# A two-layer trunk on one core: other order of small steps in attention, other queues at the start, other parts at the end

## The chip, the cores and the metric

The program runs on one core of a Trainium2 chip. The metric is device time in microseconds (us), from the first to the last instruction with what lies around them, as the median of several runs. TensorE multiplies matrices into PSUM, VectorE and ScalarE compute elementwise, GpSimd does small jobs and issues some transfers, and SyncE (SP) issues most transfers.

## The reference

Two layers over x of 256 tokens and 2048 features, all float32:

```python
for i in range(2):
    h = rms_norm(x, norm_gains[i])
    y = hgrn2_mixer(...) if i == 0 else nsa_mixer(...)
    x = x + y
return rms_norm(x, final_gain)
```

The first mixer is a gated linear recurrence with 16 heads of 128. The second is an attention with 16 heads in 4 groups and three branches (compressed, selected and window keys) whose outputs are weighted by learned gates and multiplied by silu(z). With 256 tokens there are four blocks to select from and all are taken. Each mixer has one wide input projection (2048 to 8192, and to 7216) and an output projection of 2048 x 2048. The lower bound of the first mixer's forget gate is a softmax over three rows of `hgrn_lb`.

## The kernel before, in words

**Weights.** All projections go through one loop, `flush`, over a list of pieces. A piece is a weight block of up to 128 x 1024 numbers that SP loads (`emit_load`), ScalarE casts to a rounded part hi (line 138) and VectorE subtracts to a part lo (line 148). TensorE multiplies with three products instead of one, hi times hi, hi times lo and lo times hi (lines 156, 179 and 181), so that the sum is close to float32. hi runs up to four pieces ahead of the products (`SPLIT_AHEAD`), lo three; there are four buffers of each and six of raw weights.

**Small steps.** Everything else is written as Python generators. `run` appends one to the list `steps`; `advance` gives each in the list's order one turn, up to its next `yield`. `flush` calls `advance` twice a piece, before and after its products. So a `yield` is a half step, and the order of a half step's instructions on an engine is the order of the list. Engines run their instructions in the order in which they are written; a wait holds up all that is behind it.

**Attention.** `attend(g)` handles the four heads of a group; four of them are appended to the list when the last query chunk of group 0 is done, each with a later start. A head takes four pieces: `logits` after the products of the first (three PSUM banks), `biased` and `exps` in the second, `weigh` in the third, `transposes` and `evacuate` after the products of the fourth. `transposes` fills two banks: t1 with four 128 x 128 blocks, t2 with two and the compressed branch's 47 rows. `evacuate` (lines 997 to 1012) casts the blocks to ph on ScalarE (line 1004), copies the compressed rows to pc (line 1006), and on VectorE forms the second parts pl (line 1008) and the rest of pc (lines 1009 and 1011). After two heads `values` multiplies: in one piece with the blocks of t1 and, in its last product (line 1029), with pc; in the next piece with the other blocks. The four auxiliary banks go round: for the first pair of heads of a group the next head's logits are written before the value products and both take banks that t1 and t2 held; for the second pair the value products come first.

Beside it the projections go on. A chunk of queries (`q_split`: qh on ScalarE, line 854, then ql on VectorE) or of gates (`gated`: Silu on ScalarE, line 1073, then an Exp of one column at line 1076, so that Exp's table is loaded again) ends at about the half step before an odd head's transposes.

**Start.** `load_x` loads x in eight blocks of 256 columns. The blocks and the first six weight pieces are issued by SP in turns; the two layers' gains gn by ScalarE ahead of all. TensorE runs idle products (`keep_busy`) on a tile of zeros, transposes the gains (line 1196), and x's blocks one by one (line 339); ScalarE and VectorE split x into two parts (lines 342 and 345), scaled by the gains. In the first pieces the transposes of a later x block stand between the products of an earlier piece. `setup` builds masks, the bias rows and, in its last part, the lower bounds: VectorE's lbe, an Exp on ScalarE (line 429) and five small VectorE operations.

**End.** The last 256 columns are kept back so that the first 128 tokens are finished (`finish`, lines 1156 to 1169) while TensorE still works on the other 128. `finish` adds the residual, sums squares, takes the root on GpSimd, scales x2 by it in parts, and stores three parts: 512 columns from ScalarE's queue, 512 and 1024 from SP's.

Of the kernel before, what the change touches and what calls it, by code (L numbers as in the profile page):

```python
# [8 lines left out]
F32 = mybir.dt.float32  # L9
# [3 lines left out]
AF = mybir.ActivationFunctionType  # L13
ALU = mybir.AluOpType
AX = mybir.AxisListType

P = 128
D = 2048
# [27 lines left out]
def kernel(ctx: ExitStack, tc: tile.TileContext, x, norm_gains, final_gain, rel_bias,  # L46
# [20 lines left out]
        return psa.tile([P, 512], F32, tag="aux", name="auxps")  # L67

    gn = const.tile([32, P], F32, name="gn")
    nc.scalar.dma_start(gn, norm_gains.rearrange("a (h d) -> (a h) d", d=P))  # L70
    ident = const.tile([P, P], F32, name="ident")
    make_identity(nc, ident)
    nc.scalar.activation(ident[:, 0:1], ident[:, 0:1], AF.Identity)
    mhalf = const.tile([P, 8], F32, name="mhalf")
    nc.gpsimd.memset(mhalf, -0.5)

# [248 lines left out]

    def load_x(c):
        cs = slice(c * 256, (c + 1) * 256)
        nc.sync.dma_start(xt[:, :, cs], x_rows[:, cs].rearrange("(t p) c -> p t c", p=P))

    def split_x(kts):  # L330
        if kts[0] % 2:
# [41 lines left out]
    def setup():  # L373
# [51 lines left out]
        nc.vector.tensor_max(lbm, lb3[:, 0], lb3[:, 1])  # L425
        nc.vector.tensor_max(lbm, lbm, lb3[:, 2])
        nc.vector.tensor_sub(lbe, lb3, lbm[:, None, :].to_broadcast([P, 3, NH]))
        yield
        nc.scalar.activation(lbe, lbe, AF.Exp)
        lbs = sp.tile([P, NH], F32, name="lbs")  # L430
# [487 lines left out]
        return done  # L918

    def q_split(g, a, q):  # L920
        NS["q", g, a] = [NS["p2"].tile([P, 2, S], F32R, tag="q" + part, name="q" + part, bufs=3) for part in "hl"]
        yield from split_of([q], *([t] for t in NS["q", g, a]))

# [7 lines left out]
    def attend(g):  # L931
# [64 lines left out]
        def evacuate(h):  # L996
            t1, t2 = L.pop(("t", h))
            a, hh = h // 2, h % 2
            ph, pl = pT[a]
            srcs = ((t1.rearrange("p (a t) -> p a t", a=4), slice(0, 4)),  # L1000
                    (t2[:, 0:256].rearrange("p (a t) -> p a t", a=2), slice(4, 6)))
            pc = NS["pc"][:, hh]
            for t, ks in srcs:
                nc.scalar.copy(ph[:, ks, hh, :], t)  # L1004
            for tt in range(2):
                nc.scalar.copy(pc[64:64 + NCMP, tt], t2[32 * tt:32 * tt + NCMP, 256:384])  # L1006
            for t, ks in srcs:
                nc.vector.tensor_sub(pl[:, ks, hh, :], t, ph[:, ks, hh, :].bitcast(F32))  # L1008
            nc.vector.tensor_copy(pc[0:NCMP], pc[64:64 + NCMP].bitcast(F32))
            for tt in range(2):  # L1010
                nc.vector.tensor_sub(pc[32:32 + NCMP, tt], t2[32 * tt:32 * tt + NCMP, 256:384],  # L1011
                                     pc[64:64 + NCMP, tt].bitcast(F32))

        def values(a, half):
            if half == 0:
# [53 lines left out]

    def gated(g, zs):  # L1070
        ks = [slice(4 * g + 2 * a, 4 * g + 2 * a + 2) for a in range(2)]
        for a in range(2):
            nc.scalar.activation(zs[a], zs[a], AF.Silu)  # L1073
        if g + 1 < G:

            nc.scalar.activation(NS["one"], NS["one"], AF.Exp, scale=0.0)
        yield
        yield
        for a in range(2):
            while ("out", g, a) not in NS:  # L1080
                yield
            nc.vector.tensor_mul(zs[a], zs[a], NS["o", g][:, a])
            yield
            yield
            nc.scalar.copy(yh[:, ks[a]], zs[a])
            yield
            nc.vector.tensor_sub(yl[:, ks[a]], zs[a], yh[:, ks[a]].bitcast(F32))
# [68 lines left out]
    def finish(tt, ps):  # L1156
        ms, x2, fg = FN["ms"][:, tt], FN["x2"][:, tt], FN["fg"]
        nc.vector.tensor_add(x2[:, 1792:], ps, res["x1", 4][:, tt])
        nc.vector.tensor_tensor_reduce(out=FN["sq"][:, :256], in0=x2[:, 1792:], in1=x2[:, 1792:], op0=ALU.mult,
                                       op1=ALU.add, scale=1.0 / D, scalar=ms[:, 0:1], accum_out=ms[:, 1:2])  # L1160
        nc.gpsimd.tensor_tensor(ms[:, 2:3], ms[:, 1:2], mhalf[:, :1], op=ALU.pow)
        rows, rs = out_rows[tt * P:(tt + 1) * P], ms[:, 2:3]
        nc.scalar.activation(x2[:, 0:512], x2[:, 0:512], AF.Copy, scale=rs)
        nc.vector.tensor_scalar(x2[:, 512:1024], x2[:, 512:1024], rs, None, op0=ALU.mult)
        nc.scalar.dma_start(rows[:, 0:512], x2[:, 0:512])
        nc.sync.dma_start(rows[:, 512:1024], x2[:, 512:1024])
        nc.vector.tensor_scalar(x2[:, 1024:1792], x2[:, 1024:1792], rs, None, op0=ALU.mult)
        nc.vector.scalar_tensor_tensor(x2[:, 1792:], x2[:, 1792:], rs, fg[:, 1792:], op0=ALU.mult, op1=ALU.mult)
        nc.sync.dma_start(rows[:, 1024:], x2[:, 1024:])

    def mean_so_far():
        for tt in range(2):
# [10 lines left out]
    nc.gpsimd.memset(prow, 0.0)  # L1183
    for c in range(8):
        load_x(c)
        for i in ((0, 1) if c == 0 else (c + 1,)):
            if i < RAW_BUFS:
                loaded[i] = emit_load(i)
    state["load"] = RAW_BUFS
    gp = aux_bank()  # L1190
    def keep_busy(n, m):
        for _ in range(n):
            nc.tensor.matmul(gp[:, 256:256 + P], m, m, start=True, stop=True)
# [2 lines left out]
    nc.tensor.transpose(gp[:, :32], gn, ident[:32, :32])  # L1196
    nc.vector.tensor_copy(gcol, gp[:, :32])
    start_piece(0)
    keep_busy(6, ident)
    run(setup())  # L1200
    run(norm_x())
    flush()
# [32 lines left out]
```

## Time and profile before

| | us |
|---|---|
| median of 3 runs (lowest to highest) | 986.13 (985.73 to 987.29) |
| the profiled execution | 986.4 |
| its span, first to last instruction | 984.6 |
| TensorE matmuls busy | 968.7 |
| TensorE weight loads busy | 838.5 |
| VectorE busy | 658.3 |
| ScalarE busy | 569.5 |
| GpSimd busy | 59.9 |

The profile is of one execution. A busy time is the union of an engine's instructions. Matmuls are pipelined and shown longer than the distance at which they start, so a TensorE that is shown as busy can still lose some time. In a row of the timeline the number in brackets is the time for which the engine stood idle before the instruction, with what ended it. The granted clock of TensorE is 0.998 of full speed over the span. Transfers move 178.98 MB, 182 GB/s on average.

### The profile page before, as it was taken

What the parts mean: (1) busy time and instruction counts of PE and PEld (TensorE: products, weight loads), DVE (VectorE), ACT (ScalarE), POOL (GpSimd) and SP (SyncE); (2) the same over time, 40 slices, a digit from 0 to 9 for tenths busy, and PEclk for the clock granted to TensorE, in tenths of its full rate; (3) what the DMA queues carried; (4) which work ended last, traced back from release to release, by engine and by line L of the source; (5) the groups of instructions that cost most, each with busy time, mean ns of one, the idle gap of its engine ahead of it and who ended that gap; (6) DMA issues with size and microseconds to landing.
All of it is one profiled execution on the core that took longest, in us unless ns stands there. A gap on an engine that the chain in (4) does not pass through costs nothing.

```text
span 984.6 us, 17622 instructions
## 1 busy us (share of the span) xinstructions
PE 968.7 (98%) x6735; PEld 838.5 (85%) x6735; DVE 658.3 (67%) x1275; ACT 569.5 (58%) x1056; POOL 59.9 (6%) x154
## 2 busy tenths in 40 slices
PE   9999999999999999999999999999999999999996
PEld 8888888888888888888888888998888888888886
DVE  6796478646864786465566666567777778686654
ACT  6754565456545654554455555467677776875542
POOL 3101000100010001000020000000000000000000
PEclk9999999999999999999999999999999999999999
DMA  9655565556555655566777776565555545546662
GB/s 317 201 172 151 172 192 165 157 171 193 156 166 172 186 158 163 176 222 231 234 218 207 223 229 184 157 198 170 150 152 141 158 130 160 160 130 232 204 215 96
DMA packets 141524, 178.98 MB, mean 182 GB/s; under 512 B 6016, under 2 KB 102880, under 8 KB 141312
## 3 DMA queue, kind: packets, MB, share of 16 engines
q1 hardware_dynamic: 139424, 171.86, 56.8%
q0 software_dynamic: 1680, 5.46, 2.0%
q8 instruction: 53, 0.87, 0.4%
q10 hardware_dynamic: 336, 0.54, 0.1%
q14 instruction: 31, 0.25, 0.1%
HBM read 173.62 MB, written 4.22 MB: 181 GB/s over the span
## 4 chain that ended last, share of the span: by engine, by line
PE 80%; ACT 10%; DVE 6%; issue 2%; DMA 1%; SPq 0%; POOLq 0%; ACTq 0%; POOL 0%; DVEq 0%
PE mainps L156 40%; PE mainps L179 21%; PE mainps L181 11%; PE auxps L156 3%; ACT L L970 2%; ACT hi L138 2%; PE auxps L516 2%; DVE lo L148 1%; DVE L L963 1%; ACT ph L1004 1%; ACT L L979 1%; ACT pc L1006 1%; DMA xt<-in_x_dram 1%; DVE pc L1011 1%; ACT L1073 1%
## 5 line engine op out<-in xcount | busy, mean ns | idle before, releaser
L179 PE MATMUL mainps<-xx,hi 128*128 128x512 f32 x1280 | 454.9, 398 | 0.2 <-DVE Kg L313 0.2
L138 ACT CAST hi<-raw 128x1024 fp32r<-128x1024 f32 (+3 forms) x317 | 328.0, 1039 | 206.6 <-PE mainps L156 142.8
L148 DVE TENSOR_TENSOR lo<-raw,hi 128x1024 fp32r<-128x1024 f32 (+3 forms) x317 | 379.2, 1206 | 92.1 <-ACT hi L138 91.3
L181 PE MATMUL mainps<-xx,lo 128*128 128x256 f32 x1280 | 357.6, 279 | 0.1
L179 PEld LDWEIGHTS mainps<-xx,hi 128*128 128x128 f32 x1280 | 240.2, 188 | 54.6 <-DVE Kg L313 0.6
L181 PEld LDWEIGHTS mainps<-xx,lo 128*128 128x128 f32 x1280 | 241.4, 189 | 0.6 <-DVE lo L148 0.4
L156 PE MATMUL mainps<-hi,xx 128*128 128x512 f32 (+1 forms) x704 | 209.4, 375 | 0.0
L156 PEld LDWEIGHTS mainps<-hi,xx 128*128 128x128 f32 x704 | 128.4, 188 | 23.2
L156 PE MATMUL mainps<-lo,xx 128*128 128x512 f32 (+1 forms) x352 | 131.0, 372 | 0.0
L156 PE MATMUL mainps<-hi,yh 128*128 128x512 f32 (+1 forms) x288 | 106.0, 368 | 0.0
L156 PE MATMUL mainps<-hi,yl 128*128 128x512 f32 (+1 forms) x288 | 105.4, 366 | 0.0
L156 PE MATMUL mainps<-lo,yh 128*128 128x512 f32 (+1 forms) x288 | 105.3, 366 | 0.0
L156 PEld LDWEIGHTS mainps<-lo,xx 128*128 128x128 f32 x352 | 66.1, 188 | 10.4
L156 PEld LDWEIGHTS mainps<-hi,yl 128*128 128x128 f32 x288 | 54.3, 189 | 8.8
L156 PEld LDWEIGHTS mainps<-lo,yh 128*128 128x128 f32 x288 | 54.4, 189 | 8.5
L156 PEld LDWEIGHTS mainps<-hi,yh 128*128 128x128 f32 x288 | 54.4, 189 | 8.4
L970 ACT ACTIVATE L<-L,mx 128x128 f32<-128x128 f32 (+1 forms) x96 | 37.6, 393 | 31.0 <-DVE mx L965 31.0
L313 DVE TENSOR_TENSOR zs<-mainps,zs 128x256 f32<-128x256 f32 x48 | 19.0, 421 | 33.7 <-ACT zs L311 33.7
L567 POOL COPY ST<-S 32x128 f32<-32x128 f32 x32 | 21.6, 675 | 229.8 <-DVE S L524 228.8
L524 DVE COPY_PREDICATED S<-masks,auxps 128x128 f32<-128x128 uint32 x48 | 14.6, 303 | 28.8 <-PE auxps L557 15.9
L1008 DVE TENSOR_TENSOR pl<-auxps,ph 128x512 fp32r<-128x512 f32 (+1 forms) x32 | 17.7, 557 | 22.0 <-ACT ph L1004 20.4
L311 ACT COPY zs<-mainps 128x256 f32<-128x256 f32 x48 | 16.5, 373 | 13.5 <-PE mainps L181 13.2
(257 smaller groups left out, 905.2 us busy)
## 6 DMA issues: line engine op xcount, KB each, us to landing
raw<-in_hgrn_w_in_dram SPq DMA_DIRECT2D x127, 512.0 KB, 4.0
raw<-in_nsa_w_in_dram SPq DMA_DIRECT2D x104, 512.0 KB, 3.8
raw<-in_hgrn_w_out_dram SPq DMA_DIRECT2D x32, 512.0 KB, 4.7
raw<-in_nsa_w_out_dram SPq DMA_DIRECT2D x32, 512.0 KB, 4.0
raw<-in_nsa_w_in_dram SPq DMA_DIRECT2D x10, 420.0 KB, 3.9
xt<-in_x_dram SPq DMA_DIRECT2D x8, 256.0 KB, 7.9
raw<-in_x_dram SPq DMA_DIRECT2D x4, 512.0 KB, 4.2
x_dram<-x POOLq DMA_DIRECT2D x4, 512.0 KB, 6.0
```

The source lines that it names most:

```text
L138: nc.scalar.copy(hi[:, :m], raw[:, :m])
L148: nc.vector.tensor_sub(lo[:, :m], raw[:, :m], hi[:, :m].bitcast(F32))
L156: nc.tensor.matmul(dst, a, b, start=first and n == 0, stop=last and n == 2, skip_group_check=True)
L179: nc.tensor.matmul(ps, hv[:, fs], xx[:, k].rearrange("p a t -> p (a t)"), start=k == 0, stop=False, skip_group_check=True)
L181: nc.tensor.matmul(ps[:, S:], lv[:, fs], xh[:, k], start=False, stop=k == KT - 1, skip_group_check=True)
L311: nc.scalar.copy(o, p[:, S:])
L313: nc.vector.tensor_add(o, p[:, :S], o)
L516: nc.tensor.matmul(dst[32 * b:32 * b + 32, j] if cols == 32 else dst[32 * b:32 * b + 32, :, j], k[:, cs], qs, start=True, stop=True, tile_ ...
L524: nc.vector.copy_predicated(S32, masks[:, i, None, :].to_broadcast([P, 4, 32]), bank[:, n])
L567: nc.gpsimd.tensor_copy(ST[rs, :, 0:3:2, rs], S32[rs].rearrange("p (h t) c -> p h t c", h=2))
L970: nc.scalar.activation(dst, dst, AF.Exp, bias=mx[:, i:i + 1], accum_out=sm[:, i:i + 1])
L1008: nc.vector.tensor_sub(pl[:, ks, hh, :], t, ph[:, ks, hh, :].bitcast(F32))
```

## The change

ScalarE's queue carries x's first three blocks, and the gains behind the first; the pass over one column of the identity, which also loads ScalarE's first table, is written behind these issues; two idle products fewer. The lower bound's Exp, `q_split` and `gated` each get one more `yield` ahead of them. In `evacuate` pc's copies stand right behind the first tile's cast on ScalarE, and pc's VectorE operations between the two subtractions for pl. At the end the scaling has one part of 512 columns each for VectorE, ScalarE and GpSimd and the rest for VectorE, with four stores of 512 columns on two queues.

```diff
-    nc.scalar.dma_start(gn, norm_gains.rearrange("a (h d) -> (a h) d", d=P))
     ident = const.tile([P, P], F32, name="ident")
     make_identity(nc, ident)
-    nc.scalar.activation(ident[:, 0:1], ident[:, 0:1], AF.Identity)
...
     def load_x(c):
-        nc.sync.dma_start(xt[:, :, cs], x_rows[:, cs].rearrange("(t p) c -> p t c", p=P))
+        queue = nc.scalar if c < 3 else nc.sync
+        queue.dma_start(xt[:, :, cs], x_rows[:, cs].rearrange("(t p) c -> p t c", p=P))
...
         nc.vector.tensor_sub(lbe, lb3, lbm[:, None, :].to_broadcast([P, 3, NH]))
+        yield
         yield
         nc.scalar.activation(lbe, lbe, AF.Exp)
...
     def q_split(g, a, q):
+
+        yield
...
-            for t, ks in srcs:
+
+            for n, (t, ks) in enumerate(srcs):
                 nc.scalar.copy(ph[:, ks, hh, :], t)
-            for tt in range(2):
-                nc.scalar.copy(pc[64:64 + NCMP, tt], t2[32 * tt:32 * tt + NCMP, 256:384])
-            for t, ks in srcs:
+                for tt in range(2 - 2 * n):
+                    nc.scalar.copy(pc[64:64 + NCMP, tt], t2[32 * tt:32 * tt + NCMP, 256:384])
+            for n, (t, ks) in enumerate(srcs):
                 nc.vector.tensor_sub(pl[:, ks, hh, :], t, ph[:, ks, hh, :].bitcast(F32))
-            nc.vector.tensor_copy(pc[0:NCMP], pc[64:64 + NCMP].bitcast(F32))
-            for tt in range(2):
-                nc.vector.tensor_sub(pc[32:32 + NCMP, tt], t2[32 * tt:32 * tt + NCMP, 256:384],
-                                     pc[64:64 + NCMP, tt].bitcast(F32))
+                if n == 0:
+                    nc.vector.tensor_copy(pc[0:NCMP], pc[64:64 + NCMP].bitcast(F32))
+                for tt in range(2 - 2 * n):
+                    nc.vector.tensor_sub(pc[32:32 + NCMP, tt], t2[32 * tt:32 * tt + NCMP, 256:384],
+                                         pc[64:64 + NCMP, tt].bitcast(F32))
...
     def gated(g, zs):
         ks = [slice(4 * g + 2 * a, 4 * g + 2 * a + 2) for a in range(2)]
+        yield
         for a in range(2):
             nc.scalar.activation(zs[a], zs[a], AF.Silu)
...
-        nc.scalar.activation(x2[:, 0:512], x2[:, 0:512], AF.Copy, scale=rs)
-        nc.vector.tensor_scalar(x2[:, 512:1024], x2[:, 512:1024], rs, None, op0=ALU.mult)
-        nc.scalar.dma_start(rows[:, 0:512], x2[:, 0:512])
-        nc.sync.dma_start(rows[:, 512:1024], x2[:, 512:1024])
-        nc.vector.tensor_scalar(x2[:, 1024:1792], x2[:, 1024:1792], rs, None, op0=ALU.mult)
+        parts = [slice(c, c + 512) for c in range(0, D, 512)]
+        nc.vector.tensor_scalar(x2[:, parts[0]], x2[:, parts[0]], rs, None, op0=ALU.mult)
+        nc.scalar.activation(x2[:, parts[1]], x2[:, parts[1]], AF.Copy, scale=rs)
+        nc.gpsimd.tensor_scalar(x2[:, parts[2]], x2[:, parts[2]], rs, None, op0=ALU.mult)
+        nc.sync.dma_start(rows[:, parts[0]], x2[:, parts[0]])
+        nc.scalar.dma_start(rows[:, parts[1]], x2[:, parts[1]])
+        nc.vector.tensor_scalar(x2[:, 1536:1792], x2[:, 1536:1792], rs, None, op0=ALU.mult)
         nc.vector.scalar_tensor_tensor(x2[:, 1792:], x2[:, 1792:], rs, fg[:, 1792:], op0=ALU.mult, op1=ALU.mult)
-        nc.sync.dma_start(rows[:, 1024:], x2[:, 1024:])
+        nc.sync.dma_start(rows[:, parts[2]], x2[:, parts[2]])
+        nc.scalar.dma_start(rows[:, parts[3]], x2[:, parts[3]])
...
     for c in range(8):
         load_x(c)
+        if c == 0:
+            nc.scalar.dma_start(gn, norm_gains.rearrange("a (h d) -> (a h) d", d=P))
...
+    nc.scalar.activation(ident[:, 0:1], ident[:, 0:1], AF.Identity)
...
-    keep_busy(6, ident)
+    keep_busy(4, ident)
```

## Rows read from the trace of the kernel before

**Rows 1.** Busy time by engine (and instructions) in three stretches; last clock, DMA share, GB/s

```profile
core 0: us, PE busy (x) PEld busy (x) DVE busy (x) ACT busy (x) POOL busy (x), PEclk, DMA share, GB/s
...
700.00:800.00 100.00, 97.58 (x604) 86.60 (x603) 74.83 (x208) 73.35 (x181) 2.96 (x10) 1.00 0.54 154
800.00:900.00 100.00, 95.97 (x579) 84.26 (x579) 77.85 (x208) 72.56 (x172) 2.56 (x8) 1.00 0.51 155
...
960.00:984.60 24.60, 17.23 (x144) 17.02 (x142) 10.01 (x23) 5.50 (x9) 1.14 (x2) 0.94 0.26 96
```

**Rows 2.** TensorE's own waits: what waited, for what; us in all, times, longest

```profile
PE auxps L156 <- DVE pc L1011: 2.7, 3, 0.9
PE auxps L156 <- DVE pl L1008: 2.0, 6, 0.5
PE auxps L1029 <- ACT hi L138: 1.4, 4, 0.4
```

**Rows 3.** Timeline, TensorE at 741 us: start, duration, engine, line, operation, output<-inputs

```profile
741.01 0.28 PE L156 MATMUL auxps<-Kh,ql 128*128 128x256 f32 x1
742.19 0.35 PE L156 MATMUL auxps<-ph,Vsh 128*128 128x256 f32 x1 [0.90 <-DVE pc L1011]
```

**Rows 4.** Timeline, TensorE and ScalarE, 734 to 740 us (a turn with gates)

```profile
734.51 1.28 ACT L1073 ACT_TABLE_LOAD   x1
...
735.81 1.15 ACT L1073 ACTIVATE zs<-zs 128x512 f32<-128x512 f32 x2
735.81 0.60 PE L990 MATMUL auxps<-ident,L 128*128 128x128 f32 x4
...
739.31 0.85 ACT L1004 CAST ph<-auxps 128x512 fp32r<-128x512 f32 x2
```

**Rows 5.** Timeline, ScalarE and VectorE, 767 to 772 us (a turn with queries)

```profile
767.97 0.62 ACT L854 CAST qh<-zs 128x512 fp32r<-128x512 f32 x1 [1.27 <-DVE zs L913]
...
769.45 0.84 ACT L1004 CAST ph<-auxps 128x512 fp32r<-128x512 f32 x2
...
770.05 1.24 DVE L1008 TENSOR_TENSOR pl<-auxps,ph 128x512 fp32r<-128x512 f32 x2 [0.98 <-ACT ph L1004]
```

**Rows 6.** Timeline, ScalarE, VectorE and TensorE, 32 to 36 us

```profile
32.18 0.24 ACT L429 ACTIVATE lbe<-lbe 128x48 f32<-128x48 f32 x1 [1.44 <-DVE lbe L427]
...
33.39 1.22 DVE L148 TENSOR_TENSOR lo<-raw,hi 128x1024 fp32r<-128x1024 f32 x1 [1.25 <-ACT hi L138]
...
35.01 0.50 PE L179 MATMUL mainps<-xx,hi 128*128 128x512 f32 x1 [0.24 <-DVE Kg L313]
```

**Rows 7.** Timeline of the first 12 us, and busy time in one stretch of it

```profile
0.73 0.46 ACTq L70 DMA_DIRECT2D gn<-in_norm_gains_dram  x1
...
1.05 2.93 PE L1193 MATMUL auxps<-zeros 128*128 128x128 f32 x12 [1.05 <-DVE zeros L321]
...
4.43 0.62 ACT L138 CAST hi<-raw 128x512 fp32r<-128x512 f32 x1 [1.71 <-DMA raw<-in_hgrn_w_in_dram]
...
5.07 1.68 PE L1193 MATMUL auxps<-ident 128*128 128x128 f32 x12
...
8.05 0.66 PE L339 MATMUL auxps<-ident,xt 128*128 128x128 f32 x4 [0.60 <-DMA xt<-in_x_dram]
...
11.83 0.19 PEld L181 LDWEIGHTS mainps<-xx,lo 128*128 128x128 f32 x1 [0.37 <-DVE lo L148]
...
5.50:7.00 1.50, 1.50 (x14) 1.46 (x14) 1.44 (x4) 0.91 (x2) 0.00 (x0) 1.00 0.87 246
```

**Rows 8.** Timeline and busy time at the end; GpSimd's copies (groups: busy, mean ns | idle)

```profile
979.40 0.33 SPq L1166 DMA_DIRECT2D out_dram<-fin_x  x1
...
980.32 0.33 SPq L1169 DMA_DIRECT2D out_dram<-fin_x  x1
...
980.50:983.00 2.50, 0.00 (x0) 0.00 (x0) 0.00 (x0) 0.00 (x0) 0.00 (x0) 0.73 0.99 379
...
L567 POOL COPY ST<-S 32x128 f32<-32x128 f32 x32 | 21.6, 675 | 229.8 <-DVE S L524 228.8
L409 POOL CAST masks<-mf 128x192 uint32<-128x192 f32 x1 | 0.3, 343 | 0.1
```

## The prediction

> **What bounds the kernel now.** I read the table of engine shares first: TensorE's matmuls are busy for 968.7 of 984.6 us, so an edit pays only where TensorE stands still or where the span has no matmul at all. The table by stretch gives the places [rows 1]: in the 200 us from 700 to 900 (attention beside the last projections) matmuls are busy for 97.58 + 95.97, and in the last 24.6 us for 17.23. Then I read TensorE's own waits [rows 2]. Nearly all of the idle time is of three kinds, and all of one helper, evacuate (lines 997 to 1012): waits for the second parts pl (2.0 us, 6 times), for pc before a value product starts (2.7 us, 3 times), and before line 1029 (1.4 us, 4 times; put down to a cast, but line 1029 reads pc, which is ready just then). Outside it stand 0.24 us for Kg [rows 6] and, at the start, waits for x and for lo [rows 7].
>
> A wait costs more than its idle time. In a run matmuls start 0.12 us apart, but each is shown as 0.28 us long. Between 741.01 and 742.19 [rows 3] 1.18 us pass where 0.12 would do: 1.06 are lost where the row shows 0.90. So I add 0.16 us to each wait.
>
> **The change, part by part.**
>
> *Evacuate, q_split and gated (the middle).* Take the turn at 740 us [rows 4]. The transposes run at 735.81, but ScalarE has just entered the gate's Silu: a table load of 1.28 us from 734.51, two Silus (1.15), another load back to Exp and a weight cast. ph starts only at 739.31, and pl and pc follow on VectorE. The new yield in gated puts Silu one half step later, and there attend stands earlier in the list of steps, so ScalarE is given ph and pc first. ph then starts when the first transposes are done (735.81 + 0.60, say 736.5), 2.8 us earlier. The chain behind it, which let TensorE go on at 742.19, ends at 739.4; without its two waits of this turn TensorE gets there at 742.19 - 1.06 - 0.5 = 740.6. So the waits go. What is late next is ScalarE's block of 1.28 + 1.15 + 1.28 = 3.7 us, now in front of the next weight casts; these run up to four pieces ahead of their products (SPLIT_AHEAD), so I charge nothing. Without that cover each of the three turns with a load back would cost up to 3.7 us.
>
> The turns where a query chunk ends [rows 5] have qh in front instead: ScalarE idles 1.27 us for VectorE's scaled query, casts for 0.62, and ph starts at 769.45. With the yield that leaves ph's path. VectorE gains less: it stood idle 0.98 us for ph, so pl starts 0.98 us earlier and no more. The new order inside evacuate also puts pc ahead of pl's second tile (of the 1.24 us for two, the second is some 0.45), so pc gains 1.4 us. TensorE is late there by three waits together, about 1.5 us; 0.1 may be left. pl's second tile is last now: its products are a step later, but it also holds a transposes' bank that the value product of the 740 kind of turn takes; there, as above, the whole chain ends in time.
>
> Together 2.0 + 2.7 + 1.4 = 6.1 us of idle time and 13 times 0.16 = 2.1: 8.2 us [rows 2, 3]. Bounds: 4.7, if the query turns keep their three waits of 1.5, 1.5 and 0.5; 9.2, if delays too short to show as idle time go as well. I take 8.2, the sum of the rows.
>
> *The lower bound's Exp, one half step later.* ScalarE idles 1.44 us for lbe before the Exp at 32.18; the cast behind it makes lo start at 33.39 after 1.25 us of idle VectorE; Kg's sums stand behind lo, and TensorE waits for their bank at 35.01 [rows 6]. With the Exp behind the cast, lo starts some 1.2 us sooner: 0.24 + 0.16 = 0.4 us saved (0 to 0.4). The five small operations that follow the Exp then stand behind Kg's sums, where only casts two pieces ahead are queued.
>
> *The start.* ScalarE now issues four transfers of 0.46 us from 0.73 on, then loads a table (1.28) and passes over one ident column (0.2): done at 0.73 + 1.84 + 1.48 = 4.05, before its first cast at 4.43 [rows 7]. The gains' transpose needs that column and the gains, now second on ScalarE's queue; it moves from 3.98, the end of the first idle products, to about 4.2, still beside that cast. SP's first weights go out one issue sooner. TensorE waits 0.60 us at 8.05 for x's second block and 0.37 at 11.83 for the third piece's lo. That block comes sooner, so the first wait goes; but weights and x share the transfer engines, which are busy for 0.87 of the time at 5.5 to 7 us already. Of 3 us at most 0.4 are to be won, and 0.46 by the earlier issue, while x's third block now stands beside the third weight piece and no longer behind it (256 KB at 379 GB/s [rows 8]: 0.7 us). What TensorE doesn't wait for at 8.05 it waits for at the third piece. Of the idle products, four of the twelve that take 1.68 us go, worth 0.5 at most and nothing where weights are late. I take 0.2 us saved, between 0.7 saved and 0.7 lost.
> The Trainium skill, page "Trainium Kernel Development and Optimization", section Key Constraints, says that transfers issued from several engines run on the same 16 engines and interleave, and that only issue time is saved. By it the start could win one issue, not more; the busy share of 0.87 agrees.
>
> *The end.* For the second half the first store goes out at 979.40 and the last at 980.32; from 980.5 to 983 the transfer engines are busy for 0.99 of the time, at 379 GB/s [rows 8]. The 1 MB takes 2.8 us at that rate, so here the transfer is the bound and not the scaling. The new first store still follows one VectorE part of 512 columns and goes out at the same point; four stores of 256 KB move the same bytes. GpSimd's part is of a kind that the trace does not show: at least 0.34 us (its 192-column cast), at most 2.7 (four times its 675 ns copy of 128 columns). I take 0.9, near the cast, which uses all partitions as well. The first, second and fourth stores keep the engines busy for 2.1 us, so the third has until some 2.5 us after the scaling starts. Value 0, between 0.2 saved and 0.6 lost.
> The Trainium skill, page "GPSIMD Engine Reference", section Key points, warns that GpSimd shares its memory interfaces with VectorE in a two-port mode. By it VectorE's first part could wait for GpSimd's (rival 2); no row here shows the two together.
>
> *Sum:* 8.2 + 0.4 + 0.2 + 0 = 8.8 us off the profiled execution's 986.4 is 977.6. The median of the three runs, 986.13, stands 0.3 below that execution, so on it the forecast is 977.3.
>
> **Rivals.**
> 1. VectorE takes ScalarE's place. Its lo of 1.22 us stands in front of pl in every turn, and the query turns keep their 3.5 us: 980.8. For it: VectorE is busy for 75 to 78% there [rows 1]. Against: it idled for ph, so ph was last.
> 2. The end gets longer: VectorE's first part waits for GpSimd's 0.9 us on the shared memory, and so does the first store: 978.2.
> 3. TensorE's clock. The first twelve small matmuls take 2.93 us, the next twelve 1.68 [rows 7], so the clock rises (from 1.2 to 2.4 GHz) near 5 us. If the pause before the gains' transpose and the fewer idle products let it rise later, 3 us at half speed cost 1.5: 978.8.
> 4. The yields reorder nothing, because the new generators run before attend in their half step. Then pc's earlier place helps at line 1029 alone: 1.4 + 4 times 0.16, and 0.6 for Exp and start, together 2.6: 983.5. Against: attend is put into the list before them.
> 5. Slower: the 3.7 us block behind evacuate makes weight casts late, and TensorE waits for lo in the gate turns. It decides once the cover of four pieces has shrunk below the block. Then three turns lose 3.7 and the last, without the load back, 2.4: 13.5 us, 990.8. Against: TensorE never waits for a weight part between 700 and 900 us, though ScalarE does the same work there now.
>
> **How the numbers follow.** Forecast 0.60 (976 to 979 by the bounds of start, end and middle); rivals 1 to 5: 0.16, 0.07, 0.06, 0.05, 0.03; 0.03 that new waits eat it all. The range, 975.7 to 981.2, takes in rivals 1 to 3. A measurement tells about 0.2% (2 us) from no change: faster 0.94, same 0.03, slower 0.03.
>
> **What would show it.** In the changed trace the waits for pl and pc and before line 1029 are gone or under 0.2 us each, and matmuls are busy for nearly all of the time from 700 to 890. ph starts within 1 us of the transposes in the gate turns, with the table load behind it. The wait for Kg is gone. The wait for x is gone and one for the third piece's weights has grown. From the second half's first store to the end of the span it still takes 984.6 - 979.4 = 5.2 us. I am wrong if TensorE waits for hi or lo in the gate turns, if pl's wait stays, or if the start moves by more than 0.7 us.

## The result and the profile after

| | before | after |
|---|---|---|
| median of 4 runs (lowest to highest), us | 986.11 (985.73 to 987.29) | 978.72 (978.58 to 979.1) |
| the profiled execution, us | 986.4 | 979.1 |
| its span, us | 984.6 | 977.3 |

The ratio of after to before is 0.9924, with a 95% interval from 0.9906 to 0.9941: faster, by 7.4 us. The forecast was 977.3 with a range from 975.7 to 981.2, so the time lies inside. Two terms missed in opposite directions, though, and most of this section is about them.

TensorE's own waits in the changed kernel (what waited, for what; us in all, times, longest):

```profile
PE auxps L1207 <- DMA gn<-in_norm_gains_dram: 2.2, 1, 2.2
PE auxps L1204 <- DVE zeros L319: 1.0, 1, 1.0
PE auxps L516 <- issue: 0.7, 1, 0.7
```

All waits of [rows 2] are gone, and so are the waits for Kg [rows 6], for x and for lo [rows 7]. Two are new: 2.2 us for the gains, at the very start, and 0.7 us at line 516, for which this view names no cause (more on it at the end of the part on the prediction).

Busy time by stretch (columns as in [rows 1]; the last stretch begins 24.7 us before the end, the one of before 24.6):

```profile
700.00:800.00 100.00, 100.00 (x631) 89.94 (x631) 79.66 (x227) 74.27 (x184) 2.96 (x10) 1.00 0.54 157
800.00:900.00 100.00, 100.00 (x603) 88.92 (x602) 78.30 (x206) 75.01 (x172) 2.56 (x8) 1.00 0.55 173
952.60:977.30 24.70, 17.07 (x143) 16.87 (x141) 10.35 (x23) 5.34 (x9) 4.87 (x4) 0.88 0.26 96
```

Matmuls now cover the whole stretch from 700 to 900 us; 631 start in its first half, where there were 604 [rows 1].

**The shift.** To see where the 7.3 us come from I took the same matmul in both traces (same order, same operands) and subtracted its start before from its start after. Below, "shift" is this number, "at 24 us" is by before's time, and a minus means earlier:

| stretch (time of before) | change of the shift, us | predicted |
|---|---|---|
| start, up to 24 us | +2.56 | -0.2 |
| 24 to 36 us (the Exp) | -0.50 | -0.4 |
| 36 to 700 us | +0.54 | 0 |
| 700 to 970 us (attention) | -10.15 | -8.2 |
| last matmul to the end of the span | +0.26 | 0 |
| sum | -7.30 | -8.8 |

The sum is the difference of the spans, 977.32 - 984.62.

**The start after.** Timeline, TensorE (start, duration, engine, line, operation; in brackets the idle time and what ended it):

```profile
1.04 2.93 PE L1204 MATMUL auxps<-zeros 128*128 128x128 f32 x12 [1.04 <-DVE zeros L319]
6.18 0.28 PE L1207 MATMUL auxps<-ident,gn 32*128 32x32 f32 x1 [2.22 <-DMA gn<-in_norm_gains_dram]
6.40 1.12 PE L338 MATMUL auxps<-ident,xt 128*128 128x128 f32 x4
7.31 1.91 PE L1204 MATMUL auxps<-ident 128*128 128x128 f32 x8
8.87 0.77 PE L177 MATMUL mainps<-xx,hi 128*128 128x512 f32 x1
...
9.66 0.63 PE L177 MATMUL mainps<-xx,hi 128*128 128x512 f32 x1
...
13.48 0.48 PE L177 MATMUL mainps<-xx,hi 128*128 128x512 f32 x1
...
13.91 0.40 PE L177 MATMUL mainps<-xx,hi 128*128 128x512 f32 x1
```

The issues of the same stretch (KB each, us from issue to landing; ScalarE issued x's block at 0.72 and the gains at 1.21), in the changed kernel:

```profile
xt<-in_x_dram ACTq DMA_DIRECT2D x1, 256.0 KB, 4.4
raw<-in_hgrn_w_in_dram SPq DMA_DIRECT2D x1, 256.0 KB, 4.7
gn<-in_norm_gains_dram ACTq DMA_DIRECT2D x1, 16.0 KB, 4.8
```

and in the kernel before, where SP issued x's block at 0.74 and ScalarE the gains at 0.73:

```profile
xt<-in_x_dram SPq DMA_DIRECT2D x1, 256.0 KB, 3.0
...
gn<-in_norm_gains_dram ACTq DMA_DIRECT2D x1, 16.0 KB, 2.6
```

Two things are to be read. First, the gains, 16 KB only, land at 1.21 + 4.8 = 6.0 us instead of 0.73 + 2.6 = 3.3, and x's first block at 0.72 + 4.4 = 5.1 instead of 3.7. TensorE stands still for 2.22 us. Second, the clock: the first pair of products after a block's transposes takes 0.79 us to the next pair at 8.87 (to 9.66), and 0.43 at 13.48 (to 13.91). TensorE first runs at the lower level (1.2 GHz) and then at the higher (2.4 GHz). In the trace's record of the granted clock the higher level begins at 12.40 us, and at 5.42 before; that the level ahead of it is the lower one is read from the pace of the products.

**The middle after.** The gate turn that answers to [rows 4], some 2 us later by the shift; ScalarE, then VectorE, then TensorE:

```profile
738.55 0.59 ACT L1007 CAST ph<-auxps 128x512 fp32r<-128x512 f32 x1 [1.48 <-PE auxps L992]
739.16 0.53 ACT L1009 CAST pc<-auxps 15x128 fp32r<-15x128 f32 x2
739.72 0.37 ACT L1007 CAST ph<-auxps 128x256 fp32r<-128x256 f32 x1
740.11 1.28 ACT L1078 ACT_TABLE_LOAD   x1
...
740.78 0.42 DVE L1011 TENSOR_TENSOR pl<-auxps,ph 128x256 fp32r<-128x256 f32 x1
...
742.49 0.28 PE L154 MATMUL auxps<-Kh,ql 128*128 128x256 f32 x1
742.60 0.28 PE L154 MATMUL auxps<-ph,Vsh 128*128 128x256 f32 x1
```

ph is cast as soon as the transposes are there, and the table load stands behind it. The last part, pl's second tile, ends at 741.2. The value product follows the logits after 0.11 us; before it was 1.18 from 741.01 to 742.19 [rows 3].

The query turn that answers to [rows 5]:

```profile
767.16 0.59 ACT L1007 CAST ph<-auxps 128x512 fp32r<-128x512 f32 x1 [0.23 <-PE auxps L992]
...
768.27 0.68 DVE L1011 TENSOR_TENSOR pl<-auxps,ph 128x512 fp32r<-128x512 f32 x1
...
768.59 0.63 ACT L854 CAST qh<-zs 128x512 fp32r<-128x512 f32 x1
```

qh now follows ph.

**The end after** (timeline, all engines, second half of `finish`):

```profile
971.36 0.49 DVE L1169 TENSOR_SCALAR fin_x<-fin_x,fin_ms 128x512 f32<-128x512 f32 x1 [0.69 <-POOL fin_ms L1166]
971.42 1.86 POOL L1171 TENSOR_SCALAR fin_x<-fin_x,fin_ms 128x512 f32<-128x512 f32 x1
971.76 0.78 DVE L1174 TENSOR_SCALAR fin_x<-fin_x,fin_ms 128x256 f32<-128x256 f32 x1
971.87 0.33 SPq L1172 DMA_DIRECT2D out_dram<-fin_x  x1
...
973.31 0.33 SPq L1176 DMA_DIRECT2D out_dram<-fin_x  x1
```

GpSimd needs 1.86 us for its part, so the third store goes out last, 1.44 us after the first (before, the last went out 0.92 after the first [rows 8]). From the first store to the end of the span it takes 977.32 - 971.87 = 5.45 us.

### The profile page after: what moved, and what is told of

Read it like the earlier page. It is cut to its first block, busy times and chain, and to the rows that moved or that the text cites. A ratio compares the mean times of both kernels' runs of the same rounds, so it can differ in the third digit from the quotient of the medians.

```text
span 977.3 us, 17618 instructions
## 1 busy us (share of the span) xinstructions
PE 965.7 (99%) x6731; PEld 839.6 (86%) x6731; DVE 656.7 (67%) x1275; ACT 569.1 (58%) x1056; POOL 62.9 (6%) x156
## 4 chain that ended last, share of the span: by engine, by line
PE 99%; DMA 0%; POOLq 0%; issue 0%; DVE 0%; POOL 0%; ACTq 0%
PE mainps L154 41%; PE mainps L177 31%; PE mainps L179 15%; PE auxps L154 5%; PE auxps L516 2%; PE auxps L992 1%; DMA gn<-in_norm_gains_dram 0%; PE auxps L338 0%; PE auxps L582 0%; PE auxps L609 0%; PE auxps L610 0%; PE auxps L591 0%; PE auxps L608 0%; PE auxps L633 0%; PE auxps L714 0%; PE auxps L994 0%
## 5 line engine op out<-in xcount | busy, mean ns | idle before, releaser
L1007 ACT CAST ph<-auxps 128x512 fp32r<-128x512 f32 (+1 forms) x32 | 15.4, 480 | 18.9 <-PE auxps L992 18.5
```

## The experiments

Each time is a median beside runs of the kernel before on the same chip (985.9 to 986.1 us in all of them).

### What the new start costs

**old_start**: the changed kernel with the start of before.

```diff
+    nc.scalar.dma_start(gn, ...)            # ahead of all, as before
+    nc.scalar.activation(ident[:, 0:1], ident[:, 0:1], AF.Identity)
...
-        queue = nc.scalar if c < 3 else nc.sync
-        queue.dma_start(xt[:, :, cs], ...)
+        nc.sync.dma_start(xt[:, :, cs], ...)
...
-        if c == 0:
-            nc.scalar.dma_start(gn, ...)
...
-    nc.scalar.activation(ident[:, 0:1], ident[:, 0:1], AF.Identity)
...
-    keep_busy(4, ident)
+    keep_busy(6, ident)
```

> The changed kernel with the whole start as before (x and weights on SP, gains first on ScalarE, six idle products). Theory: the new start costs 2.5 us, so this takes 976.3 and TensorE's first product is back at 6.5 us. Rival: the start is worth 0.2 us at most and the missing 1.4 us of the forecast lie in attention or at the end: 978.7 to 978.9.

Measured: 975.97 us (975.56 to 976.06), ratio 0.9893 [0.9877, 0.991]. The shift at 24 us is -0.01. So the new start costs 978.72 - 975.97 = 2.75 us, near the +2.56 of the trace (the difference of the medians also holds what differs later in the executions, as the wait at line 516); the rival, that the start is worth 0.2 us at most, is out. The first product did not come back to 6.5 us as expected, and a row of this run tells more:

```profile
5.05 2.50 PE L1202 MATMUL auxps<-ident 128*128 128x128 f32 x12
7.30 0.48 PE L179 MATMUL mainps<-xx,hi 128*128 128x512 f32 x1
```

In this execution the clock rose only at 7.14 us (5.42 before) and the first product starts at 7.30 where it was 6.50; still nothing is lost at 24 us. A lateness of 0.8 us is covered, for TensorE would have waited 0.60 for x and 0.37 for lo anyway [rows 7].

**start_only**: the kernel before with the new start alone.

```diff
-    nc.scalar.dma_start(gn, ...)
...
-    nc.scalar.activation(ident[:, 0:1], ident[:, 0:1], AF.Identity)
...
-        nc.sync.dma_start(xt[:, :, cs], ...)
+        queue = nc.scalar if c < 3 else nc.sync
+        queue.dma_start(xt[:, :, cs], ...)
...
+        if c == 0:
+            nc.scalar.dma_start(gn, ...)
...
+    nc.scalar.activation(ident[:, 0:1], ident[:, 0:1], AF.Identity)
...
-    keep_busy(6, ident)
+    keep_busy(4, ident)
```

> The kernel before with the new start alone. Theory: 2.5 us slower than before (988.6), less up to 0.4 if the late start also changes the wait for Kg. Rival: within 0.5 us of before.

Measured: 989.81 us (988.84 to 990.56), ratio 1.0033 [1.002, 1.0046]; slower than before. The shift at 24 us is +1.94, with the same wait for the gains (2.3 us) and the clock up at 9.60 us. By itself this part of the change is a loss. It is 3.7 us by the medians where 2.5 were expected; in the trace the rest comes later, +0.9 near 171 us (the wait of line 516, here line 515), +0.3 in the last turn of attention and +0.44 behind the last matmul.

**gn_first**: the changed kernel, the gains issued ahead of x's first block.

```diff
+    nc.scalar.dma_start(gn, ...)            # first on ScalarE
...
-        if c == 0:
-            nc.scalar.dma_start(gn, ...)
```

> The changed kernel with the gains issued first on ScalarE, ahead of x's first block; all else as changed. Theory (the gains are late because they stand behind x's block in one queue): they land near 3.3 us again; x's first block, which shares the engines with the weights, still lands near 5.2, so TensorE starts its products near 7.5 instead of 8.9 and the kernel takes about 977.3. Rival (two queues side by side make everything late, whatever the order): the gains land after 5 us still, 978.7.

Measured: 977.76 us (977.51 to 978.51), ratio 0.9913 [0.9898, 0.9928]; shift at 24 us +1.24. The gains land at 3.8 us, but x's first block at 5.75, and TensorE waits 1.25 us for it; the clock rises at 8.97 us. Half of the loss is gone. The time lies between the expected 977.3 and the rival's 978.7: all came later than expected (the first product at 8.28 us, not 7.5), but the rival, gains after 5 us whatever the order, is out.

**more_idle**: the changed kernel, 16 idle products on zeros.

```diff
-    keep_busy(6, zeros)
+    keep_busy(16, zeros)
```

> The changed kernel with 16 instead of 6 idle products on zeros ahead of the gains' transpose, so that TensorE doesn't stand idle while it waits for the gains. Theory: about half of the start's loss is the clock, which rose at 12.4 us instead of 5.4; it now rises near 5.4, the first products start about when they did or 0.3 earlier and run at full speed: 977.5. Rival: the clock's share is hidden behind late weights, and only the gains' lateness counts: 978.7, though the clock rises early.

Measured: 976.97 us (976.74 to 977.67), ratio 0.9905 [0.989, 0.992]; shift at 24 us +1.05. Timeline, TensorE:

```profile
1.04 5.24 PE L1204 MATMUL auxps<-zeros 128*128 128x128 f32 x32 [1.04 <-DVE zeros L319]
6.34 0.22 PE L1207 MATMUL auxps<-ident,gn 32*128 32x32 f32 x1
6.48 0.65 PE L338 MATMUL auxps<-ident,xt 128*128 128x128 f32 x4
6.97 1.06 PE L1204 MATMUL auxps<-ident 128*128 128x128 f32 x8
8.01 0.50 PE L177 MATMUL mainps<-xx,hi 128*128 128x512 f32 x1
```

The time is below the expected 977.5. The gains are no earlier here (their transpose stands at 6.34, in the changed kernel at 6.18). TensorE runs idle products up to that point instead of standing still, the clock is at its higher level from 4.01 us, and the x transposes take 0.65 us instead of 1.12, the first product 0.50 instead of 0.77. So 2.56 - 1.05 = 1.5 us are the clock alone: of all that the late gains do, the pause they leave is the dear part.

**gn_first_idle** and **gn_first_idle11**: both repairs, with 16 and with 11 idle products.

```diff
+    nc.scalar.dma_start(gn, ...)            # first on ScalarE
...
-        if c == 0:
-            nc.scalar.dma_start(gn, ...)
...
-    keep_busy(6, zeros)
+    keep_busy(16, zeros)                    # the other kernel: keep_busy(11, zeros)
```

> The changed kernel with both repairs of the start: gains issued ahead of x's first block on ScalarE's queue, and 16 idle products on zeros instead of 6. If the start's loss has two causes that add (late gains with x's first block, and the late rise of the clock), the shift of TensorE at 24 us is 0.2 to 0.7 us (changed kernel 2.56; 1.24 with the gains first alone; 1.05 with the idle products alone), full clock from about 4 to 5 us, and the time is 976.3 to 976.9. Rival: both repairs take away the same wait (whichever comes first hides the other), then the shift stays at 1.0 or more and the time is 977.0 to 977.7. What is left in the first case is x's first block itself, which landed at 5.75 instead of 3.74 us behind the gains.

> As the kernel with the gains first and 16 idle products, but with 11: with 16 the idle products ended at 6.6 us, a microsecond after x's first block had landed (5.55), so the repair was itself in the way. With 11 they end at about 5.7 us. If late data and the late rise of the clock are the two causes and add, the shift of TensorE at 24 us is 0.1 to 0.5 us (0.87 with 16, 1.24 with 6, 2.56 in the changed kernel), the first product starts at 7.4 to 7.9 us, and the time is 976.2 to 976.9. Rival: what is left is the weights and x's later blocks, which the transfer engines bring no sooner, then the shift at 24 us stays at 0.8 to 1.2 although the first product starts earlier: 976.9 to 977.4.

Measured: 977.18 us (976.67 to 978.02), ratio 0.9913 [0.9897, 0.993], and 976.74 us (976.63 to 976.86), ratio 0.9901 [0.9885, 0.9918]. The shift at 24 us is +0.87 and +0.95. Both expected shifts were missed: the two repairs don't add; whichever is made, the other has little left. With 11 the first product started at 7.77, as expected, and it did not help, which is what the rival says. What is left can be read from the chain of work that ended last, up to 13 us (start, duration, what); with 11 idle products:

```profile
1.65 7.28 DMA xt<-in_x_dram
8.98 0.67 PE auxps L339 x4
...
11.48 1.24 DVE lo L147
12.76 0.39 PE mainps L180
```

and in the kernel before:

```profile
2.20 5.80 DMA xt<-in_x_dram
8.05 0.67 PE auxps L339 x4
...
10.55 1.24 DVE lo L148
```

Both chains begin with x's second block and go over its transposes, the split of x and the third piece's parts to the product for which TensorE waits. The block is issued 0.55 us sooner and lands 0.93 later (8.93 instead of 8.00 us), and from there all stands 0.93 later, the shift at 24 us too. In more_idle the block lands at 9.04, 1.04 later, and the shift is +1.05. The likely reason is the order of the issues: SP, which no longer issues x's first blocks, issues the third piece's weights (512 KB) at 1.64 us instead of 2.68. In the six traces with this order the weights land first (7.6 to 8.1 us) and then x's second block (8.4 to 9.0); in the seven with the start of before the block lands first (6.6 to 8.1) and then the weights (9.2 to 9.6). So the loss of the changed kernel has two parts: some 1.5 us for the pause and the clock, and some 1.0 for x's second block, which neither repair reaches. No run moved this block alone ahead of those weights.

**x12_act**: the middle and the Exp changed, the end and the start as before, but for x's second and third block, which ScalarE issues.

```diff
-        nc.sync.dma_start(xt[:, :, cs], ...)
+        queue = nc.scalar if c in (1, 2) else nc.sync
+        queue.dma_start(xt[:, :, cs], ...)
```

> The kernel before with the middle and the Exp changed, gains first on ScalarE and x's first block first on SP as before; only x's second and third blocks are issued by ScalarE. If the part of the new start that hurts is the first block and the gains alone, the wait for x's second block (0.6 us at 8.05 before, 1.2 in the same kernel with all of x on SP) goes or falls under 0.3, the shift at 24 us is between -0.5 and 0, and the time is 975.4 to 976.3. Rival: blocks issued earlier on a second queue take bandwidth from the gains, the first block and the first weights whatever their order, then the gains land over 0.5 us later than 3.31 and the shift at 24 us is +0.3 to +1.5: 976.5 to 977.8.

Measured: 982.29 us (981.72 to 982.85), ratio 0.9962 [0.9947, 0.9977]; outside both expectations. Timeline, ScalarE's queue and TensorE:

```profile
4.49 1.90 ACTq L329 DMA_DIRECT2D xt<-in_x_dram  x2
6.43 0.62 ACT L138 CAST hi<-raw 128x512 fp32r<-128x512 f32 x1 [3.71 <-DMA raw<-in_hgrn_w_in_dram]
...
12.62 0.69 PE L340 MATMUL auxps<-ident,xt 128*128 128x128 f32 x2 [3.43 <-DMA xt<-in_x_dram]
```

The two blocks are not issued early but late: the first issue stands at 4.49 us and holds up the cast behind it (6.43; 4.43 before [rows 7]); x's second block then comes after 12.5 us. The first weights, issued at 1.22, landed at 4.47, just ahead of that issue, and in the trace's record this issue waits for the semaphore that tells of that landing. The second issue, at 6.01, waits in the same way for the next weights' semaphore (5.99). The kernel therefore tests nothing of what it was made for, the sharing of bandwidth. It does show what 3.43 us without matmuls do: the shift at 24 us is +6.15, and the clock, up at 7.27 us, is at its higher level for good only from 17.51 us.

### What the middle gains, and from which part

**yields_only**: the kernel before with the yields in `q_split` and `gated`.

```diff
     def q_split(g, a, q):
+        yield
...
         ks = [slice(4 * g + 2 * a, 4 * g + 2 * a + 2) for a in range(2)]
+        yield
```

> The kernel before with the new yields of q_split and gated alone; evacuate in its old order. Theory: the order of the half step is what counts; the gate turns lose their waits entirely (3 times 1.6 and 0.9) and the query turns about 1 us each, since pl starts earlier by the 0.98 us that VectorE idled for ph: 986.1 less 8 is 978; small waits before line 1029 stay in the query turns. Rival (the yields reorder nothing, only pc's place helps): 986.

**evac_only**: the kernel before with the new order inside `evacuate` (the hunks of that function in the change, nothing else).

```diff
-            for t, ks in srcs:
+            for n, (t, ks) in enumerate(srcs):
                 nc.scalar.copy(ph[:, ks, hh, :], t)
+                for tt in range(2 - 2 * n):
+                    nc.scalar.copy(pc[64:64 + NCMP, tt], ...)
...
```

> The kernel before with evacuate's new order alone, no new yields. Theory: pc comes 0.45 us sooner, so the four waits before line 1029 shrink from 0.53 to 0.1 and the waits at a bank of the 740 kind of turn stay, because the chain's end is the same: 2 us less than before, 984. Rival (pc's place is the main part): 981 or less.

**gated_only**: the kernel before with the yield in `gated` alone.

```diff
         ks = [slice(4 * g + 2 * a, 4 * g + 2 * a + 2) for a in range(2)]
+        yield
```

> The kernel before with the yield in gated alone. If each yield mends its own kind of turn, the three waits for pc at line 156 (2.7 us in all) go, those of the query turns (pl at line 156, line 1029) stay, and of the 10.15 us that both yields give between 700 and 970 us some 4 to 5 come: time 981 to 982. Rival: the turns are coupled (what the query turn leaves late is what the gate turn waits for), then the pc waits stay in part (over 1 us in all) and under 3 us come: 983 to 984.5.

Measured: yields_only 976.33 us (976.0 to 976.64), ratio 0.99 [0.9885, 0.9914]; evac_only 980.43 (979.75 to 980.87), 0.9941 [0.9926, 0.9955]; gated_only 979.97 (979.41 to 980.07), 0.9938 [0.9923, 0.9952]. All three came out lower than expected (978, 984, and 981 to 982); evac_only fits its rival, 981 or less. The change of the shift by turn (Q: a query chunk ends; G: gates; us):

| kernel | Q 711 | G 741 | Q 770 | G 801 | Q 831 | G 860 | last 891 | sum |
|---|---|---|---|---|---|---|---|---|
| after, old_start, yields_only | -0.49 | -1.74 | -1.60 | -1.78 | -1.61 | -1.87 | -1.07 | -10.15 |
| gated_only | +0.03 | -1.74 | -0.02 | -1.78 | -0.01 | -1.87 | -1.07 | -6.46 |
| evac_only | -0.49 | -0.56 | -1.43 | -0.54 | -1.44 | -0.58 | -1.07 | -6.11 |

The turns don't depend on each other: the yield in `gated` mends its own kind and the last turn (also of gates) to the last digit, and nothing else; it gives 6.46 us where 4 to 5 were expected. TensorE's waits with it,

```profile
PE auxps L1029 <- ACT hi L138: 1.0, 3, 0.4
PE auxps L156 <- DVE pl L1008: 0.7, 2, 0.3
```

are the query turns' waits. The yield in `q_split` was not run alone; as the difference of the first two rows it gives 3.69 us. The new order in `evacuate` mends nearly all of the query turns, the whole of the last turn and a third of the other gate turns, in which it leaves

```profile
PE auxps L156 <- DVE pl L1009: 2.4, 3, 0.8
```

because there ph itself starts late behind Silu and the two table loads (738.92 us in the turn at 741), which no order inside `evacuate` changes. With both yields it adds nothing, and the small waits before line 1029 that were expected to stay with the yields alone are not there. The expectation that the parts add, and that `evacuate` alone gives 984, was wrong: the two are two cures for the same waits.

### The end, and the change without its start

**end_no_pool**: old_start, with VectorE in GpSimd's place.

```diff
-        nc.gpsimd.tensor_scalar(x2[:, parts[2]], x2[:, parts[2]], rs, None, op0=ALU.mult)
...
-        nc.vector.tensor_scalar(x2[:, 1536:1792], x2[:, 1536:1792], rs, None, op0=ALU.mult)
+        nc.vector.tensor_scalar(x2[:, 1024:1792], x2[:, 1024:1792], rs, None, op0=ALU.mult)
```

> Start as before, all else as changed, but at the end VectorE scales the third part too (columns 1024 to 1792 in one operation, some 0.6 us) and GpSimd none; four stores on two queues as changed. Theory (GpSimd's part is what costs, by its own 1.86 us and by slowing VectorE beside it, 0.78 us for 256 columns): the third store goes out before 980.3's counterpart, the end is as short as with three stores or 0.1 shorter, 975.6. Rival (four smaller stores cost by themselves): 976.0.

Measured: 976.10 us (975.47 to 976.7), ratio 0.9897 [0.9882, 0.9912]; old_start, with GpSimd's part, 975.97: no difference that these runs can tell, so neither the expected 975.6 nor the rival's 976.0 is decided. VectorE's row:

```profile
969.24 0.61 DVE L1174 TENSOR_SCALAR fin_x<-fin_x,fin_ms 128x768 f32<-128x768 f32 x1
```

768 columns take 0.61 us here, and 256 columns took 0.78 in the changed kernel, beside GpSimd. VectorE's two other operations beside GpSimd's part were not slower (0.49 and 0.47 us; 0.49 and 0.48 here). So one of three is slowed, and it is not on the path.

**best**: the middle and the Exp changed; start and end as before.

```diff
         nc.vector.tensor_sub(lbe, lb3, lbm[:, None, :].to_broadcast([P, 3, NH]))
+        yield
...
     def q_split(g, a, q):
+        yield
...
-            for t, ks in srcs:
+            for n, (t, ks) in enumerate(srcs):
...
     def gated(g, zs):
         ks = [slice(4 * g + 2 * a, 4 * g + 2 * a + 2) for a in range(2)]
+        yield
```

> Start and end as before; evacuate, q_split, gated and the lower bound's Exp as changed. Theory: the new end costs 0.26 us (GpSimd's part took 1.86 us and its store goes out last), so this takes 975.7, 0.2 to 0.3 less than with the new end, and from the last product to the end 7.4 us instead of 7.6. Rival (the end is bound by the transfer alone): the same as with the new end, 976.0.

Measured: 976.86 us (975.96 to 977.22), ratio 0.9904 [0.9888, 0.9921]. Shift at 24 us +0.20, from 700 to 970 us -10.15. The expected 975.7 and the rival's 976.0 were both missed. The time from the last matmul to the end of the span, with the end as before, is 7.39 or 7.40 us in before, evac_only and x12_act but 7.82 or 7.83 in start_only, yields_only, gated_only and best, though the last store goes out 3.1 us behind the last matmul in all of them; with the new end it is 7.64 to 7.84. So the end costs and gives nothing that these runs can tell. The fastest kernels are this one, yields_only, old_start, end_no_pool and gn_first_idle11, 975.97 to 976.86 with intervals that overlap: the change without its start, or with its start repaired, beats both kernels.

## Why the prediction was right, and where it was wrong

**The middle: right in mechanism, a fifth too small.** "So the waits go" held for every wait of [rows 2]; ph starts with the transposes' end in the gate turns, the table load stands behind it, and the block of 3.7 us makes no weight cast late (no wait for hi or lo from 700 to 900 us: rival 5 falls, as do rival 1, whose waits for pl are gone, and rival 4, for the yields reorder all that was forecast). Two steps were too small. The term "13 times 0.16" took one product's lateness for the price of a wait, but the product that has waited is also followed later: after 770.80, a product that waited 0.34 us, the next one starts at 771.02, 0.22 later instead of 0.12. Aligned product by product, that wait cost 0.61 + 0.10 us. So the 13 waits cost 0.26 each above their idle time, not 0.16: 6.1 + 13 times 0.26 = 9.5. And the products that wait for ph in two query turns, one with 0.2 us idle and one with none shown, cost 0.33 and 0.29 and were not in the sum. 10.15 came out instead of 8.2, above my upper bound of 9.2. The reason given for two parts of the change was also too wide: I credited `evacuate`'s order with pc's gain in the query turns, and the yields alone give all of it.

**The Exp: right.** 0.50 measured, 0.4 forecast; the wait for Kg is gone, and comes back where the Exp is as before (0.3 in yields_only and start_only).

**The start: this step failed.** By the prediction's own sign, a start that moves by more than 0.7 us, this part is wrong. The step read: "it moves from 3.98, the end of the first idle products, to about 4.2", and "I take 0.2 us saved, between 0.7 saved and 0.7 lost". The transpose moved to 6.18 and the start lost 2.56. The wait for x at 8.05 did go, but the one for the third piece's lo went too instead of growing, for TensorE was late enough for both. The working counted when the gains are issued (0.48 us later) and not when they land (2.7 us later). I had bounded the effect of the order on x's blocks by the busy share of the transfer engines, and not asked the same of the gains, which are small but which everything at the start waits for. A second sentence failed as well, "That block comes sooner, so the first wait goes": x's second block lands at 8.77 us instead of 8.00, behind the third piece's weights (7.59; 9.36 before), which SP now issues earlier. By more_idle the first failure costs some 1.5 us, through the pause and the clock, and the second some 1.0.

The Trainium skill, page "Trainium Kernel Development and Optimization", section Key Constraints, has transfers from several engines interleave on the same 16. The trace agrees: the 16 KB of gains land 0.9 us after the 256 KB block ahead of them in their queue, and 0.2 after the weights that SP issued at about the same time (1.17 + 4.7 = 5.9). I used this rule only to bound what the start could win, and did not ask what it could cost a transfer that stands behind or beside large ones.

**Rival 3 happened, beside the forecast.** The clock rose later (12.40 instead of 5.42 us) and more_idle shows 1.5 us for it, the price that I had given (1.5). Its trigger, the pause before the gains' transpose, is the one that I had named, but I had put that transpose at 4.2 us and so the pause near nothing; it was 2.22 us. I had given this rival 0.06 as one case among others, though the forecast and it were not exclusive. That its time, 978.8, is nearly the measured one is luck: it holds neither the 1.0 us of x's second block nor the middle's surplus. And that the time came near 977.3 at all is luck too: without the middle's surplus of 1.95 us it would be 980.7, still inside the range.

**The end: value 0 held within what can be told.** The changed kernel's tail is 0.26 us longer, but the old end varies by 0.44, and so the 5.45 us from the first store to the end don't tell against the 5.2 that were to stay. GpSimd's part took 1.86 us, not 0.9, inside the bounds of 0.34 and 2.7. Rival 2 was wrong in its place: VectorE's first part, which the first store waits for, took 0.49 us; it was the next one that was slow.

**Not foreseen:** +0.54 us between 36 and 700 us, with the wait of 0.7 us at line 516 (near 171 us of before's time). The wait comes and goes: 0.8 us in start_only, 1.0 in evac_only, 0.5 in end_no_pool and in gn_first, none in the nine other kernels' traces. Its row in the changed kernel:

```profile
174.52 0.27 PE L516 MATMUL auxps<-QL,KL 128*32 128x32 f32 x7 [0.73 <-issue]
```

The traces hold a likely cause, which no run tested. Each has a transfer of 16 KB of the kind "instruction" near this place. In the five with the wait it lands 0.2 to 0.7 us after the small products of line 516 have begun (here at 173.17, they begin at 172.59), and the product that waited starts 1.30 to 1.47 us after the landing. In the nine without the wait it lands 0.3 to 1.4 us before these products begin. So TensorE seems to wait there for the program itself; what makes this transfer late in some executions stays open.

## What to carry to other kernels

When a transfer is moved, follow it to its landing and not to its issue, and follow what moves up in the queue that it left: here 16 KB behind 256 KB landed 2.7 us later, and x's second block landed 0.8 us later behind a weight piece that had moved up. At the start a pause of TensorE cost twice here, once as idle time and once as the half clock after it, so that idle products up to the first real operand gave back 1.5 us. In a region bound by one engine's waits, price a wait by the shift of the same matmul in two traces and not by the idle time shown (here 0.26 us more for each wait), and test the parts one at a time: here two cures for the same waits gave 6.1 and 10.15 us alone and 10.15 together.

## What the runs showed of the hardware

- VectorE beside GpSimd: a scaling of 256 columns took 0.78 us while GpSimd scaled 512 (1.86 us), and 768 columns 0.61 without GpSimd; VectorE's other two operations beside it (512 and 256 columns, 0.49 and 0.47 us) were not slower. The Trainium skill, page "GPSIMD Engine Reference", section Key points, says that the two share their interfaces to SBUF and contend in some modes of VectorE; the trace agrees for the one operation, and does not tell in which mode each ran.
- The clock's rise differs between executions with the same start: with the start of before the higher level begins at 4.33 (best), 5.42 (before) and 7.14 us (old_start). The last cost nothing at 24 us (shift -0.01), for TensorE would have waited for x anyway.
- A transfer's issue can itself stand still: x12_act's second block was issued at 4.49 us on an engine that was idle from 2.72 on. The timeline shows no wait for it; in the trace's record the issue waits for the semaphore of another queue's transfer, which landed at 4.47. In the changed kernel SP's fourth block of x stands in the same way until x's first block has landed (issued at 5.17, landed at 5.16).
- A wait of TensorE that is put down to nothing can be one for the program: the five waits at line 516 end 1.30 to 1.47 us after a 16 KB transfer of instructions has landed (likely, not tested).
